# Block products for q and k of seven heads, spilled to DRAM, with the attention moved behind them

## The chip, the core and the metric

The kernel runs on one core of a Trainium2 chip. The metric is the device time of one execution in microseconds. Of the kernel before, three runs took 1871.21, 1871.85 and 1873.03 us; the median, 1871.85 us, is what changes are measured against. TensorE (PE in the profile) multiplies matrices out of SBUF into eight PSUM banks, VectorE (DVE) and ScalarE (ACT) work on tiles in SBUF and PSUM, GpSimd (POOL) does some elementwise work and issues transfers, and SyncE (SP) issues most transfers. Each engine takes its instructions in order.

## What is computed

One layer of an encoder on 512 tokens of width 2048, in float32. The part that the change concerns is the first half:

```python
h = rms_norm(x, pre_mix_g[l])
z = h @ w_in[l]                                   # 2048 x 4096: q | k | v | u, 1024 columns each
q = z[..., :ATTN_WIDTH]                           # 8 heads of 128
k = z[..., ATTN_WIDTH:2 * ATTN_WIDTH]
v = z[..., 2 * ATTN_WIDTH:3 * ATTN_WIDTH]
u = z[..., 3 * ATTN_WIDTH:]
a = chunked_attention(q, k, v, rel_bias[l])       # softmax(q k^T * scale + bias) v per head
p = multiscale_pool(u, pool_w[l], pool_scale[l])  # trailing means over 2/4/8/16, minus token, a 256 x 256 map
m = jnp.concatenate([a, p], axis=-1) @ w_o[l]
x = x + rms_norm(m, post_mix_g[l])
# then h @ w_up, a depthwise convolution, a gelu gate, @ w_down, and a second residual
```

## The kernel before

**Numbers.** Each factor of a product is split into a rounded high part and the rest (`split`, L133: the high part by ScalarE, the rest by VectorE). A product is three matmuls, high by high, high by low, low by high (`mm3`, L150). Where seven block products are used, `mm2` (L156) makes each product from a wide matmul (high of the weights by high and low of the activations, 512 columns) and a narrow one (low of the weights by high, 256 columns).

**Seven block products.** A product of two 2 x 2 block matrices needs eight block products, or seven if sums and differences of blocks are multiplied instead. The kernel before does this in the up-projection (`Factors`, `seven` and `keep`, from L1066) and in the products with w_o and w_down, but not in the projection by w_in. There the blocks are halves of the 2048 inputs, halves of the 512 tokens, and two groups of 128 output columns; the three sums of activations are made once, the sums of weights for each group of columns, by transfers that add.

**Order of the work.** TensorE's order is written out in the program; the other engines' instructions are ordered by a planner among those that are ready. `Weights` (L55) loads and splits weights in a given list, four ahead of use, into five raw tiles and eight split tiles.

1. x is loaded in 16 parts, scaled by its gain and split; q and k of head 0 are multiplied meanwhile (L335 to L349). The squares of x for the norm are summed by ScalarE and GpSimd (L365 to L373); the factor 1/rms is applied later, to the results (`R` along tokens, `rt` per token).
2. `v_group(0)` (L413): v of heads 0 to 3 as four PSUM banks of 128 tokens by 512 columns.
3. For each head h: q (`project`, L399, 48 matmuls), transposes of the softmax of an earlier head (`turn`, L462), scores of the previous head (`scores`, L437), k (48 matmuls), and values of an earlier head (`values`, L474). So between a head's scores and its transposes two projections and one head's values run. The second group of v stands at head 5.
4. Eight projections u, with the pool's running sums on VectorE (`pool_keep`, L485) and its map (`pool_mix`, L508), and the last heads' attention among them.
5. The product with w_o, the norm, then the second half of the layer.

In the softmax, VectorE adds the bias to the scores, GpSimd sets a masked corner by a memset (L450), VectorE takes the maximum, ScalarE the exponential, VectorE scales. Sums of blocks of w_o and w_down are made in DRAM by transfers spread over the stages (`sums_in_dram`, L296): plain copies on SyncE's queue, adding ones on GpSimd's queue, each waiting for the transfer that it builds on.

The rows of w_in are read where they lie: a tile for 128 columns consists of pieces of 512 bytes.

Of the kernel before, what the change touches and what calls it, by code (L numbers as in the profile page):

```python
# [54 lines left out]
class Weights:  # L55


    def __init__(self, specs, load, ahead):
        self.specs, self.load, self.ahead, self.tiles, self.used = specs, load, ahead, [], 0

    def prefetch(self, n=None):
        upto = min(len(self.specs), self.used + (self.ahead if n is None else n))
        while len(self.tiles) < upto:
            self.tiles.append(self.load(*self.specs[len(self.tiles)]))
# [11 lines left out]
def encoder_layer(ctx: ExitStack, tc: tile.TileContext, x, xT, vecs, rel, post_mix, post_ffn,  # L76
                  w_in, pool_w, w_o, w_up, w_down, out):
# [13 lines left out]
    acc = mixing.enter_context(tc.tile_pool(name="acc", bufs=1))  # L91
# [51 lines left out]
    def load_w(name, src, a, b):  # L143
        n = a * b
        raw, hi, lo = raw4(name + "r"), w4(name + "h"), w4(name + "l")
        load_w.last = nc.sync.dma_start(raw[:, :n].rearrange("p (a b) -> p a b", a=a), src).ins
# [30 lines left out]
    def new_hT(name):  # L177

        return [new_pair(f"{name}{i}", 4, S) for i in range(4)]

    def blk(hT, kb, sl=slice(None)):
        return tuple(hT[kb // 4][:, part, kb % 4, sl] for part in range(2))


# [8 lines left out]
    def g_both(gT, kb):  # L193
        v = gT[kb // 4][:, kb % 4]
        return v[:, 1:3, :].rearrange("p a b -> p (a b)"), v[:, 0:4:3, :]

# [19 lines left out]
    def halves(name, w, c0, a, b):  # L216
        n = KD // a
        return [(f"{name}_{i}", rows(w, i * a * P, c0, a, b), a, b) for i in range(n)]

    def head_cols(what, h):  # L220
        return {"q": 0, "k": ATTN, "u": 3 * ATTN}[what] + h * P

    def qk_specs(h):
        return halves(f"q{h}", w_in, head_cols("q", h), 8, P), halves(f"k{h}", w_in, head_cols("k", h), 8, P)

    def v_specs(i):
        return halves(f"v{i}", w_in, 2 * ATTN + i * 512, 2, 512)
# [26 lines left out]

    def v_and_ready_specs(g):
        specs = v_specs(g)
        for n in range(4 if g == 0 else 2):
            (cc, i), j = READY[2 * g + n // 2], n % 2
            specs.insert(3 * n + 2, (f"rw{cc}{i}_{j}", first_block(cc, i - 1, 0)[:, 2 * j:2 * j + 2, :], 2, 512))
        return specs  # L260

    def keep_ready(g, n):
        if 2 * g + n // 2 >= len(READY):
            return
        (cc, i), j = READY[2 * g + n // 2], n % 2
# [4 lines left out]
    for h in range(1, HEADS):  # L270
        q, k = qk_specs(h)
        specs += q + k
        if h == 5:
            specs += v_and_ready_specs(1)
    for g in range(4):
        for j in range(2):
            specs += halves(f"u{2 * g + j}", w_in, head_cols("u", 2 * g + j), 8, P)
        if g:
            specs += pm_spec(g - 1)
    for i in WO:  # L280
# [9 lines left out]
    weights = Weights(specs, load_w, 4)  # L290

# [34 lines left out]
    R = RR[:, 0, :]  # L326
    rt = const.tile([P, NT], F32, name="rt")
    xt = [acc8(f"xT{i}", "AABB"[i]).rearrange("p (a b) -> p a b", a=4) for i in range(4)]
    hT = new_hT("hT")
# [5 lines left out]
    for kb in range(KD):  # L335
        i, o = divmod(kb, 8)
        nc.sync.dma_start(xt[kb // 4][:, kb % 4, :], xT[kb * P:(kb + 1) * P, :])
        for what in "qk":
            if kb in chunks:
                raw, hi, lo = first[f"{what}0_{i}"]  # L340
                sl = slice(o * P, (o + chunks[kb]) * P)
                nc.sync.dma_start(raw[:, sl].rearrange("p (a b) -> p a b", b=P),
                                  rows(w_in, kb * P, head_cols(what, 0), chunks[kb], P))
                split(hi[:, sl], lo[:, sl], raw[:, sl])
        last_split = split(*blk(hT, kb), xt[kb // 4][:, kb % 4, :], col(V_PREMIX, kb))
        for what in "qk":
            _, hi, lo = first[f"{what}0_{i}"]
            sl = slice(o * P, (o + 1) * P)
            mm3(ps0[what], (hi[:, sl], lo[:, sl]), blk(hT, kb), kb == 0, kb == KD - 1)  # L349
    weights.prefetch(3)  # L350
    nc.sync.dma_start(vec[:, V_CONV:], vecs[:, V_CONV:])


# [5 lines left out]
    with tc.tile_pool(name="p1", bufs=2, reuse_waits="tile") as p1:  # L359
# [3 lines left out]
        ssum = t512("bias", bufs=1)  # L363

        with tc.issue_after(last_split):  # L365
            for kb in range(KD):
                sq = t512("tmp")
# [1120 lines left out]
```

## Time and profile before

| | |
|---|---|
| median of the runs | 1871.85 us (1871.21 to 1873.03) |
| profiled execution: time and span | 1869.37 and 1867.6 us |
| granted TensorE clock | 0.999 |
| VectorE, ScalarE, GpSimd busy | 1437.1, 1020.2, 297.8 us |
| HBM read and written | 361.44 and 96.47 MB |

The profile is one execution, taken by the hardware profiler. A page gives the busy time of each engine, the chain of work that ended last (followed back from the last instruction), and groups of instructions; other views give the timeline, the waits and tables of stretches of time. A group's row has the source line, the engine, the operation, the tile written and those read, the shape, the count, then busy time and the mean of one in ns, then the idle time before and what ended it. A timeline's row has the start and the length in us. Matmuls overlap in the pipeline, so the time of one is read from the starts of consecutive ones and not from the length in its row.

### The profile page before, as it was taken

How to read it: one execution, taken by the hardware profiler on the slowest of the kernel's cores; microseconds unless marked ns; L12 is line 12 of the kernel's file. 1: busy time of each engine (PE TensorE's matmuls, PEld its weight loads, DVE VectorE, ACT ScalarE, POOL GpSimd, SP SyncE). 2: the span in 40 equal slices, each digit the busy share in tenths (PEclk: the TensorE clock that was granted, in tenths of full speed). 3: DMA queues.
4: the chain of work that ended last, by engine and by line, in shares of the span. 5: the costliest groups of instructions: out<-in, count | busy, mean ns of one | idle time of the engine just before them, and what ended most of it. 6: DMA issues, size and time to landing. Idle time of an engine off the chain costs nothing.

```text
span 1867.6 us, 24890 instructions
## 1 busy us (share of the span) xinstructions
PE 1857.1 (99%) x9486; PEld 1590.2 (85%) x9486; DVE 1437.1 (77%) x1631; ACT 1020.2 (55%) x1287; POOL 297.8 (16%) x400
## 2 busy tenths in 40 slices
PE   9999999999999999999999999999999999999998
PEld 7888888888889888888888888888888888888886
DVE  5555445577598988888888888888887899899875
ACT  6433333346455566656666565565655665565553
POOL 4301011100000121221212212122121001111101
PEclk9999999999999999999999999999999999999999
DMA  8899599997794689898888988988889977877785
GB/s 298 248 255 233 163 253 252 246 251 255 225 306 180 184 203 206 199 205 204 201 206 194 207 208 198 208 196 207 208 174 299 352 221 174 199 206 180 173 245 143
DMA packets 181751, 409.20 MB, mean 219 GB/s; under 512 B 11456, under 2 KB 62528, under 8 KB 176320
## 3 DMA queue, kind: packets, MB, share of 16 engines
q0 software_dynamic: 52112, 156.78, 43.9%
q1 hardware_dynamic: 129520, 250.84, 40.1%
q8 instruction: 74, 1.21, 0.3%
q14 instruction: 45, 0.37, 0.1%
HBM read 361.44 MB, written 96.47 MB: 245 GB/s over the span
## 4 chain that ended last, share of the span: by engine, by line
PE 98%; DVE 1%; ACT 1%; DMA 0%; SPq 0%; issue 0%; POOL 0%; DVEq 0%; POOLq 0%; ACTq 0%
PE qa L159 16%; PE qa L165 8%; PE qg L159 8%; PE qg L165 4%; PE qd L159 4%; PE pa L153 4%; PE pa L154 4%; PE pa L151 4%; PE m L154 3%; PE m L151 3%; PE m L153 3%; PE qd L165 2%; PE pg L153 2%; PE pg L154 2%; PE pg L151 2%; PE u L151 2%
## 5 line engine op out<-in xcount | busy, mean ns | idle before, releaser
L159 PE MATMUL qa<-gT,wfh 128*128 128x512 f32 x984 | 246.4, 392 | 0.0
L135 ACT ACTIVATE wfh<-wx 128x1024 fp32r<-128x1024 f32 x164 | 173.8, 1060 | 129.0 <-PE qg L159 46.4
L136 DVE TENSOR_TENSOR wfl<-wx,wfh 128x1024 fp32r<-128x1024 f32 x164 | 200.4, 1222 | 51.7 <-ACT wfh L135 37.4
L159 PEld LDWEIGHTS qa<-gT,wfh 128*128 128x128 f32 x984 | 177.0, 189 | 31.7
L1106 POOL DMA_DIRECT2D wx<-in_w_up x122 | 104.6, 857 | 500.4 <-DVE wfl L136 464.5
L159 PE MATMUL qg<-h,wfh 128*128 128x512 f32 x656 | 162.1, 389 | 0.0
L159 PEld LDWEIGHTS qg<-h,wfh 128*128 128x128 f32 x656 | 122.9, 188 | 25.4
L136 DVE TENSOR_TENSOR bl<-b,bh 128x2048 fp32r<-128x2048 f32 x56 | 127.1, 2286 | 18.6 <-ACT bh L135 11.7
L135 ACT ACTIVATE wfh<-wy 128x1024 fp32r<-128x1024 f32 x82 | 86.9, 1060 | 93.1 <-PE qg L159 52.8
L165 PE MATMUL qa<-gT,wfl 128*128 128x256 f32 x984 | 137.7, 283 | 0.0
L135 ACT ACTIVATE bh<-b 128x2048 fp32r<-128x2048 f32 x56 | 106.1, 1913 | 57.0 <-DVE b L870 22.8
L165 PEld LDWEIGHTS qa<-gT,wfl 128*128 128x128 f32 x984 | 129.4, 191 | 3.4
L151 PE MATMUL pa<-bh,ah 128*128 128x512 f32 x320 | 124.5, 389 | 0.0
L153 PE MATMUL pa<-bl,ah 128*128 128x512 f32 x320 | 124.5, 389 | 0.0
L154 PE MATMUL pa<-bh,al 128*128 128x512 f32 x320 | 124.5, 389 | 0.0
L136 DVE TENSOR_TENSOR wfl<-wy,wfh 128x1024 fp32r<-128x1024 f32 x82 | 100.1, 1220 | 7.3 <-ACT wfh L135 3.0
L165 PEld LDWEIGHTS qg<-h,wfl 128*128 128x128 f32 x656 | 89.5, 190 | 6.4
L136 DVE TENSOR_TENSOR wfl<-wz,wfh 128x1024 fp32r<-128x1024 f32 x41 | 50.2, 1224 | 54.1 <-PE qa L159 52.8
L165 PE MATMUL qg<-h,wfl 128*128 128x256 f32 x656 | 91.5, 282 | 0.0
L159 PE MATMUL qa<-h,wfh 128*128 128x512 f32 x328 | 82.1, 392 | 0.0
L159 PE MATMUL qd<-gT,wfh 128*128 128x512 f32 x328 | 81.0, 389 | 0.0
L938 POOL DMA_DIRECT2D sum<-part x30 | 36.2, 1207 | 261.7 <-DVE part L924 190.1
(543 smaller groups left out, 4549.9 us busy)
## 6 DMA issues: line engine op xcount, KB each, us to landing
wx<-in_w_up POOLq DMA_DIRECT2D x122, 512.0 KB, 6.1
b<-in_w_down SPq DMA_DIRECT2D x32, 1024.0 KB, 7.0
wx<-in_w_up SPq DMA_DIRECT2D x43, 512.0 KB, 5.4
wz<-in_w_up SPq DMA_DIRECT2D x41, 512.0 KB, 5.7
wy<-in_w_up SPq DMA_DIRECT2D x41, 512.0 KB, 4.6
wy<-in_w_up POOLq DMA_DIRECT2D x41, 512.0 KB, 6.6
sum<-part POOLq DMA_DIRECT2D x38, 512.0 KB, 7.7
wt<-in_w_o POOLq DMA_DIRECT2D x16, 1024.0 KB, 12.8
```

Source lines behind the costliest of these rows:

```text
L135: rounded = nc.scalar.activation(hi, src, AF.Copy)
L136: rest = nc.vector.tensor_sub(lo, src, f32(hi))
L151: nc.tensor.matmul(ps, l[0], r[0], start=first, stop=False, skip_group_check=onto)
L153: nc.tensor.matmul(low, l[0], r[1], start=False, stop=False, skip_group_check=onto)
L154: nc.tensor.matmul(ps, l[1], r[0], start=False, stop=last, skip_group_check=onto)
L159: nc.tensor.matmul(ps, w[0][:, kb], pairs[kb][0], start=fresh and not kb, stop=last, skip_group_check=not fresh)
L165: nc.tensor.matmul(ps[:, sl], w[1][:, kb], pair[:, sl], start=False, stop=last, skip_group_check=not fresh)
L938: nc.gpsimd.dma_start(dest, v, accum_op=ALU.add)
L1106: nc.gpsimd.dma_start(self.raw[k, what], self.block(k, m, kh), accum_op=ALU.add)
```

## The change

- q and k of heads 1 to 7 are made by seven block products for each head; the two groups of 128 columns are q and k of the head. The activations' sums are made from x while the first group of v is multiplied. The weights' sums are made by VectorE.
- The results of a head (before the factor 1/rms) are written to DRAM (`zqk`), with k negated as the block scheme gives it; the factor is applied when they are read back, by GpSimd (`load_head`). The results of v are written and read back in the same way (`vd`), and so are the pool's results of the first three groups (`pooled`).
- All attention runs after the last block product: three heads within the second group of v, five within the projections u. The pool's running sums move from VectorE to GpSimd, and several tiles of this stage get one buffer and not two.
- The second and fourth quarter of the activations (the later half of the tokens, first half of the inputs) are overwritten by a difference during the block products and restored from x afterwards.
- w_in comes as packed blocks, so that a row of a tile lies as 4 KB in one piece.

The diff, cut; a line that is only "..." marks what is left out:

```diff
     def v_and_ready_specs(g):
...
+    READY_AT = {0: (7,), 1: (3, 4, 5, 6, 7)}
...
+    z0 = raw4("z0").rearrange("p (a b) -> p a b", a=2)
+    nc.scalar.activation(z0[:, 0], ps0["q"], AF.Copy)
+    nc.vector.tensor_scalar_mul(z0[:, 1], ps0["k"], -1.0)
+    nc.gpsimd.dma_start(zqk[0], z0)
...
+    def v_spill(i, ps):
+        for p in range(2):
+            v = raw4(f"vs{p}").rearrange("p (a b) -> p a b", a=2)
+            for t in range(2):
+                nc.scalar.activation(v[:, t], ps[2 * p + t], AF.Copy)
+            nc.gpsimd.dma_start(vd[i][:, 2 * p:2 * p + 2, :], v)
+
+    def scaled(q):
+        for kb in range(4 * q, 4 * q + 4):
...
+                    nc.scalar.activation(sq, v, AF.Square)
+                    nc.gpsimd.tensor_add(ssum, sq, ssum)
+                nc.scalar.activation(v, v, AF.Copy, scale=col(V_PREMIX, kb))
+            yield
...
+    def x_sums():
+        for i in range(2):
+            yield from scaled(2 + i)
+            yield from scaled(i)
...
+            nc.vector.tensor_sub(a22, a22, a21)
+            keep(5, a22)
+            nc.vector.tensor_sub(a21, a11, a21)
+            differences.append(a21)
+            nc.vector.scalar_tensor_tensor(a11, a22, -1.0, a11, op0=ALU.mult, op1=ALU.subtract)
+            keep(6, a11)
+            nc.vector.scalar_tensor_tensor(a12, a11, -1.0, a12, op0=ALU.mult, op1=ALU.subtract)
+            keep(3, a12)
...
+    class Pairs:
...
+        def make(self, k, i):
...
+            split(hi, lo, {3: y, 7: y, 2: z}.get(i, x))
+            if i == 1:
+                nc.vector.tensor_add(x, x, w)
+            elif i == 5:
+                nc.vector.tensor_add(x, x, y)
+            elif i == 6:
+                nc.vector.tensor_add(x, x, z)
+            elif i == 3:
+                nc.vector.tensor_add(y, y, w)
...
+    def qk_product(k, i):
+        w = pairs.get()
+        if i in FIRST:
+            qk_banks[k, BANK[i]] = bank(f"q{BANK[i]}_{k}")
+        mm2(qk_banks[k, BANK[i]], w, [factor_of(ms, i, kb) for kb in range(8)], i in FIRST, i in TURNED)
...
+        elif i == 4:
...
+            nc.vector.tensor_add(z[:, 0, :T], one[:, 0, 0], one[:, 0, 1])
+            nc.vector.tensor_add(z[:, 1].rearrange("p (a b) -> p a b", a=2), m[:, :, 0], m[:, :, 1])
+            nc.scalar.activation(z[:, 0, T:], a[:, T:], AF.Copy)
+            nc.vector.tensor_add(z[:, 0, T:], a[:, :T], z[:, 0, T:])
+            nc.gpsimd.dma_start(zqk[k + 1], z)
...
+    for k, i in [at for at in pairs.order if at[0] is not None]:
+        if k == pairs.n - 1 and i in (7, 4):
...
+            next(steps)
+        qk_product(k, i)
+        qk_keep(k, i)
...
+        if (k, i) == (pairs.n - 1, 7):
+            restore()
+        if i in (3, 7, 4) and (k, i) != (0, 3):
+            more_sums(1)
...
+        def load_head(h):
+            state["bias", h] = t512("bias", bufs=1)
+            nc.sync.dma_start(state["bias", h], rel[h])
+            v = p1.tile([P, 2, S], F32, tag="zq", bufs=1, name="zq")
+            nc.sync.dma_start(v, zqk[h])
+            nc.gpsimd.tensor_mul(v, v, RR)
+            pair = [p1.tile([P, 2, S], F32R, tag="qk" + p, bufs=1, name="qk" + p) for p in "hl"]
+            split(*pair, v)
+            state["qk", h] = [tuple(p[:, n, :] for p in pair) for n in range(2)]
...
                 nxt = p1.tile([P, WIDE], F32, tag="us", bufs=2, name="us")[:, :PAD + S]
-                nc.vector.tensor_add(nxt[:, step:], cur[:, step:], cur[:, :PAD + S - step])
+                nc.gpsimd.tensor_add(nxt[:, step:], cur[:, step:], cur[:, :PAD + S - step])
...
+        load_head(0)
+        v_load(0)
+        for h in range(3):
+            run(3 if not h else 1)
+            scores(h)
+            more_sums(1)
+            run(1)
+            if h:
+                values(h - 1)
+            more_sums(1)
+            run(2)
+            turn(h)
+        run(1)
+        v_spill(1, psv)
...
+        for j in range(8):
+            ps = project(f"u{j}", mid(2 if j == 0 else j + 1) if j not in (1, 7) else None)
+            if 1 <= j <= 5:
+                turn(j + 2)
+                if j < 5:
+                    scores(j + 3)
+            if j in (2, 4, 6):
+                pool_mix(j // 2 - 1, spill_mix)
+            if j < 7:
+                pool_keep(j // 2, j % 2, ps)
+                more_sums(2 if j == 6 else 1)
...
+    qk_blocks = w_in[0][:, :2 * ATTN].reshape(2, 8, P, 2, HEADS, P).transpose(4, 3, 0, 2, 1, 5)
```

`run(n)` advances the second v by n steps of 12 matmuls; two of its 16 steps run before the last two block products. `mid(h)` is called in the middle of a projection u and issues the values of head h (and, once, the scores of head 3).

More of the change, by code (lines that the diff above doesn't have):

```diff
@@ new lines, in encoder_layer @@
+    pairs = Pairs()
+    psv = [bank(f"v0_{t}") for t in range(NT)]
+    sums_of_x = x_sums()
+    for n, _ in enumerate(v_steps(0, psv)):
+        for _ in range(2):
+            next(sums_of_x, None)
+        if n == 9:
+            for i, v in enumerate(differences):
+                split(*(hT[i][:, :, at, :] for at in AT[1]), v)
+            early_x.close()
+            p0 = mixing_w.enter_context(tc.tile_pool(name="p0", bufs=1, reuse_waits="tile"))
+    weights.limit = len(specs)
+    psr = bank("R")
@@ L389, in encoder_layer @@
         state = {}
-        def keep(what, h, ps):
-            f = t512("tmp")
-            nc.vector.tensor_mul(f, ps, R)
-            hi, lo = t512(what + "h", F32R), t512(what + "l", F32R)
-            split(hi, lo, f)
-            state[what, h] = hi, lo
         def project(name, between=None):
```

347 lines of the change are left out of this document (213 added, 134 removed).

## The prediction

> **What bounds the kernel now.** I read the page's busy times first, then the chain that ended last, then what TensorE waited for.
>
> ```profile
> span 1867.6 us, 24890 instructions
> PE 1857.1 (99%) x9486; PEld 1590.2 (85%) x9486; DVE 1437.1 (77%) x1631; ACT 1020.2 (55%) x1287; POOL 297.8 (16%) x400
> PE 98%; DVE 1%; ACT 1%; DMA 0%; SPq 0%; issue 0%; POOL 0%; DVEq 0%; POOLq 0%; ACTq 0%
> PE q L151 <- ACT q_0h L135: 0.3, 1, 0.3
> PE q L153 <- DVE hT L139: 0.3, 1, 0.3
> ```
>
> TensorE is busy for 99% of the span, the chain is 98% TensorE, and apart from the first instruction its named waits are two of 0.3 us at the start. So time is saved only by giving TensorE fewer columns, and lost only by a new wait of TensorE. Next I look at what one head costs on TensorE now, from the timeline, and at what seven block products cost where the kernel already uses them (its up-projection), from the chain and from a table of stretches.
>
> ```profile
> 108.74 1.09 PE pt L468 x10
> 111.61 0.39 PE L151 MATMUL k<-hT,k_0h 128*128 128x512 f32 x1
> ...
> 122.51 0.39 PE L151 MATMUL a<-pth,vh 128*128 128x512 f32 x1
> ...
> 135.51 1.09 PE pt L468 x10
> ```
>
> The 48 matmuls of k take 122.51 - 111.61 = 10.90 us, 0.227 us each; q is the same work, so q and k of a head take 21.80 us. The transposes `pt` come once a head, 135.51 - 108.74 = 26.77 us apart, so one head's attention takes 26.77 - 21.80 = 4.97 us of TensorE: 1.09 the transposes, and the scores and the values, which have equal columns, 1.94 each.
>
> ```profile
> 667.44 1.91 PE qa L165 x16
> ...
> 1388.78 1.91 PE qa L165 x16
> ```
> ```profile
> core 0: us, PE busy (x) PEld busy (x) DVE busy (x) ACT busy (x) POOL busy (x), PEclk, DMA share, GB/s
> 667.40:1388.80 721.40, 721.40 (x4147) 637.13 (x4146) 600.74 (x706) 440.30 (x537) 156.06 (x186) 1.00 0.89 203
> ```
>
> In the up-projection a block of the same size as q and k of a head takes seven products of 8 wide and 8 narrow matmuls, 112 in all. The 721.4 us hold 4147 / 112 = 37 blocks, 19.50 us each, with TensorE busy throughout at clock 1.00, VectorE busy 83% and ScalarE 61%.
>
> **The change, part by part.** *The products.* Heads 1 to 7 fall from 21.80 to 19.50 us: 7 x 2.30 = 16.1 us off TensorE. Head 0, v, the pool projections u and every matmul of the attention stay, as many and as wide, so this is the whole gain. Beyond it, 4 KB rows can win at most the two waits of 0.3 us at the start, because no other wait of TensorE is a transfer; I take 0, bounds 0 and -0.6.
>
> *The sums before the products.* While v of the first four heads runs, ScalarE now squares and scales x, and splits the sums as well as the weights.
>
> ```profile
> 22.40:72.70 50.30, 50.30 (x225) 41.65 (x224) 19.87 (x17) 24.63 (x33) 29.45 (x23) 1.00 0.80 262
> L368 ACT ACTIVATE tmp<-xT 128x512 f32<-128x512 f32 x16 | 9.8, 628 | 8.3 <-POOL bias L372 8.1
> L135 ACT ACTIVATE wfh<-wx 128x1024 fp32r<-128x1024 f32 x164 | 173.8, 1060 | 129.0 <-PE qg L159 46.4
> L136 DVE TENSOR_TENSOR wfl<-wx,wfh 128x1024 fp32r<-128x1024 f32 x164 | 200.4, 1222 | 51.7 <-ACT wfh L135 37.4
> ```
>
> From the last split of x to the end of v are 50.3 us. ScalarE's list: 32 instructions of 0.63 (16 squares, 16 scalings) = 20.2; 9 weight splits, 6 splits of sums, 2 of differences and 4 of the first factors, 21 x 1.06 = 22.3; together 42.5 us, 84%. VectorE: 21 splits x 1.22 and 8 sums, costed like a split, 35.4 us. Both fit; lower bound 0. The upper: the third and fourth pieces of x must be finished before the z weights land in their place. If that is 3 us late, the second product waits 3 us. I take 0, since both engines keep over 7 us free.
>
> *The stage of the products.* Per head VectorE makes 7 splits and 4 sums of 1024 (11 x 1.22 = 13.4) and, after the products, the adds whose prices stand in these rows.
>
> ```profile
> L1182 DVE TENSOR_TENSOR z<-zm 128x512 f32<-128x512 f32 x41 | 28.3, 691 | 1.4
> L1184 DVE TENSOR_TENSOR z<-qa,z 128x256 f32<-128x256 f32 x41 | 17.1, 417 | 0.3 <-ACT z L1183 0.3
> ```
>
> That is 4 x 0.69 + 2 x 0.42 = 3.6, in all 17.0 of 19.5 us, 87%. The up-projection ran without a TensorE wait at 83%, and there the weight sums were made by transfers, here by VectorE, which shortens their chain. Cost 0. If VectorE's cover went, a head would take VectorE's time and not 19.5.
>
> *The move of the attention.* All eight heads now run in what is left of the second v (14 of its 16 steps of 12 matmuls, 14 x 2.73 = 38.2 us), the eight u (8 x 10.90) and three pool mixes (3 x 2.73): with 8 x 4.97 that is 173.4 us on TensorE. What a head's transposes wait for is its softmax, and its cover shrinks. Today two projections and one head's values, some 23.7 us, lie between a head's scores and its transposes. After the change three v steps do for head 0 (8.2 us), three steps and one head's values for heads 1 and 2 (10.1), and one u and values for heads 4 to 7 (12.8); head 3 has half a u more. I measure the softmax from the last scores matmul to the last scaling.
>
> ```profile
> 111.37 0.40 PE L154 MATMUL s<-kh,ql 128*128 128x512 f32 x1
> 138.15 0.40 PE L154 MATMUL s<-kh,ql 128*128 128x512 f32 x1
> ```
> ```profile
> 120.37 0.48 DVE L457 TENSOR_SCALAR s<-s,rs 128x512 f32<-128x512 f32 x1
> 148.21 0.49 DVE L457 TENSOR_SCALAR s<-s,rs 128x512 f32<-128x512 f32 x1
> ```
> ```profile
> 140.80 1.24 POOL L303 DMA_DIRECT2D wt<-in_w_o  x1 [25.04 <-DMA wt<-in_w_o]
> 141.54 0.92 POOL L450 MEMSET s<- 64x64 f32 x4
> ```
>
> With the next matmul issued 0.23 us later, head 1 needs 120.85 - 111.60 = 9.2 us and head 2 148.70 - 138.38 = 10.3: there GpSimd's mask memsets stood behind a DRAM sum that was waiting for a transfer. So head 0 is late by 9.2 - 8.2 = 1.0 us, and heads 1 and 2, by the dearer chain, by 0.2 each. Heads 3 to 7 have 2.5 us or more in hand: 0. Behind a waiting transpose stand the v or u matmuls and thus everything else of TensorE.
>
> GpSimd's load grows: each head's q and k times 1/rms (128x1024, reading SBUF), and the running sums of the pools.
>
> ```profile
> L372 POOL TENSOR_TENSOR bias<-tmp,bias 128x512 f32<-128x512 f32 x14 | 23.8, 1700 | 3.3 <-ACT tmp L368 2.6
> L493 DVE TENSOR_TENSOR us<-u 128x527 f32<-128x527 f32 x8 | 5.7, 707 | 0.4
> ```
>
> The multiplication isn't in the trace; twice the row gives 3.4 us. The pool sums go from 0.71 on VectorE to some 1.75 on GpSimd, 16 of them within the stage. One memset caught behind one multiplication makes the dearer chain 13.7 us: upper bounds 5.5 us for head 0, 3.6 each for heads 1 and 2, 0.9 each for 4 to 7. I stay with the measured chains.
>
> *Spills and their return.* A head's result goes out and comes back; only head 0's return is near its use.
>
> ```profile
> sum<-part POOLq DMA_DIRECT2D x38, 512.0 KB, 7.7
> bias<-in_rel SPq DMA_DIRECT2D x8, 256.0 KB, 5.8
> ```
>
> Head 0 was written long before. Its load needs room that the sums of x give up after the last 6-product, some 11 us before the last product ends, and scores(0) stands 8.2 us behind that end. Load (the slower row, 7.7), multiplication 3.4 and split 2.3 make 13.4 of 19.2 us: 0. If the load had to wait for the last head's spill (adds of z 1.5, spill 7.7, then 13.4), scores(0) would be 22.6 - 8.2 = 14.4 us late; that is the upper bound. The spills, the packed loads and the reload of half of x add transfers to queues that TensorE does not wait for today.
>
> *The sum.* 1869.37 (the profiled run, 1.8 above its span) - 16.1 + 1.0 + 0.4 = 1854.7. The median of the runs, 1871.85, lies 2.5 above that run: **1857.2 us**.
>
> [...] Some of this slows where GpSimd and VectorE overlap, and the trace shows it:
>
> ```profile
> L372 POOL TENSOR_TENSOR bias<-tmp,bias x14: 1288/1598/2244, 25.7 to 53.0; 128x512 f32<-128x512 f32 x14
> 33.44 1.49 DVE L136 TENSOR_TENSOR v_2l<-v_2r,v_2h 128x1024 fp32r<-128x1024 f32 x1 [2.79 <-ACT v_2h L135]
> 53.20 2.18 DVE L136 TENSOR_TENSOR rw_0l<-rw_0r,rw_0h 128x1024 fp32r<-128x1024 f32 x1 [2.79 <-ACT rw_0h L135]
> ```
>
> The same GpSimd add takes 1.29 to 2.24 us, and a split beside it up to 2.18 where 1.22 is usual. [...]
>
> **The rivals.** *One, VectorE becomes the bound in the attention stage.*
>
> ```profile
> L452 DVE TENSOR_REDUCE nm<-s 128x1 f32<-128x128 f32 (+3 forms) x32 | 15.0, 470 | 5.0 <-POOL s L450 5.0
> L136 DVE TENSOR_TENSOR ptl<-pt,pth 128x512 fp32r<-128x512 f32 (+3 forms) x32 | 14.2, 483 | 0.1
> L448 DVE SCALAR_TENSOR_TENSOR s<-s,bias 128x128 f32<-128x128 f32 (+3 forms) x32 | 14.0, 480 | 0.0
> L457 DVE TENSOR_SCALAR s<-s,rs 128x128 f32<-128x128 f32 (+3 forms) x32 | 12.2, 382 | 0.3
> ```
>
> These four groups are 55.4 us for eight heads; eight splits of q and k 9.8, 29 weight splits 35.4, and some 27 for pools, v and x (an estimate from the same prices by size): about 128 of 173.4 us. GpSimd's reads are 8 x 3.4 + 16 x 1.75 = 55 us. If every one stopped VectorE, VectorE would need 183 us, 10 more than TensorE: 1871.85 - 16.1 = 1855.8 is the time without a wait, so 1855.8 + 10 = 1866, and up to 1870 with late softmaxes. For it: the 2.18. Against: the 17 VectorE instructions of the stretch from 22.4 to 72.7 us, in which those adds ran, took 19.87 us, 1.17 each, no more than a split alone.
>
> *Two, head 0's return is late* by the bound above: 1855.8 + 14.4 = 1870.2, or about 1864 for half of it. For it speaks that space is tight and loads share one queue; against, the 5.8 us in hand.
>
> *Three, slower: the softmax is held up by GpSimd at every head.* Its four memsets are short but in order with multiplications, pool sums and DRAM sums. With three of them behind 1.75 us each the chain is 9.2 + 5.3 = 14.5 us, and TensorE waits 6.3 + 4.4 + 4.4 + 4 x 1.7 = 21.9 us: 1855.8 + 21.9 = 1877.7. It decides against the change from a chain of some 13.5 us. For it: head 2's four memsets in a row. Against: one such case cost 1.1 us, not 5.3.
>
> *Four, the seven products bring nothing*, because VectorE's 17.0 us a head stretch to 21.8: 1872. Against it speaks the up-projection's stretch.
>
> **How the numbers follow.** The forecast's case (waits of 0 to 6 us in all, 1854 to 1862) gets 0.56, rivals one and two 0.12 each, three 0.14, four 0.06. About 0.2% (3.7 us) is what a measurement of this kernel can tell from no change. Faster (below 1868.1) are the forecast, rival two and 0.07 of rival one, together 0.75; the rest of one and all of four are the same, 0.11; slower 0.14. The range starts at 1854.2 (no wait, the start's 0.6 us gained, 1 us of scatter) and ends at 1870.5, which leaves out rival three, rival four and the worst of the others.
>
> **What would show it.** Right: per head 112 matmuls in 19.5 us without gaps in the stage of the products; VectorE there near 87%; TensorE's waits of about 1 us before head 0's transposes and almost none later; a GpSimd multiplication of about 3.4 us. Wrong: product periods over 20 us, waits of the scores for the split of q and k (rival two), waits of the transposes at most heads with memsets behind GpSimd work (three), splits of 2 us and more all through the u stage (one). More than 6 us of such waits refutes the sum.

## The result, and the profile after

The changed kernel takes 1963.69 us (median of four runs, 1958.3 to 1965.19) against 1871.72 us (four runs beside them): 1.0485 times the time before, with a 95% interval of 1.0464 to 1.0506. The forecast was 1857.2 us, faster. The first view is the page of the changed kernel: busy times, TensorE's busy tenths and its granted clock in 40 slices of 49 us, and the chain.

```profile
span 1960.8 us, 25466 instructions
PE 1865.3 (95%) x9598; PEld 1598.1 (81%) x9598; DVE 1530.2 (78%) x1704; ACT 1083.5 (55%) x1376; POOL 357.0 (18%) x446
PE   9977947979999999999999999999999999999998
...
PEclk9988968989999999999999999999999999999999
...
PE 79%; DMA 7%; DVE 6%; issue 3%; ACT 2%; POOL 2%; SPq 0%; DVEq 0%; POOLq 0%; ACTq 0%
```

TensorE now stands still for 1960.8 - 1865.3 = 95.5 us, where it was 10.5. Nearly all of it lies in the slices 3 to 11, the stage that the change rewrote, and there the granted clock falls as well, to the digit 6 in the sixth slice. The chain, which was 98% TensorE, holds 7% of transfers and 6% of VectorE. The stretches of the rewritten stage show where (the columns after the range: length, busy us of each engine with its instructions, granted clock, share of the DMA engines, GB/s):

```profile
80.00:240.00 160.00, 136.44 (x748) 117.86 (x747) 108.58 (x116) 67.03 (x82) 18.38 (x19) 0.94 0.89 248
240.00:290.00 50.00, 21.08 (x93) 17.52 (x92) 19.90 (x34) 14.69 (x25) 7.99 (x41) 0.71 0.85 263
290.00:400.00 110.00, 98.66 (x468) 83.38 (x468) 73.10 (x137) 49.76 (x95) 33.39 (x45) 0.93 0.78 241
400.00:440.00 40.00, 29.54 (x149) 25.53 (x148) 23.55 (x47) 14.66 (x31) 13.52 (x22) 0.87 0.88 226
440.00:550.00 110.00, 103.07 (x447) 83.91 (x446) 72.50 (x92) 56.16 (x75) 23.94 (x34) 0.97 0.73 220
550.00:1940.00 1390.00, 1387.27 (x7300) 1196.38 (x7299) 1159.84 (x1195) 818.92 (x971) 227.81 (x260) 1.00 0.83 211
```

So 23.6 us are lost in the block products (80 to 240), 28.9 where the attention begins, 28.7 in the rest of the attention and at w_o, and 2.7 behind. What TensorE waited for (total, times, longest):

```profile
PE s L156 <- ACT qkh L138: 28.2, 1, 28.2
PE pt L688 <- DVE s L677: 20.1, 4, 10.5
PE qg L170 <- DVE wfl L139: 8.9, 1, 8.9
PE qa L170 <- DVE wfl L139: 8.8, 1, 8.8
```

**The sum that closes.** TensorE's full-clock work fell by 7 x (21.80 - 19.57) = 15.6 us (the 19.57 is measured further down). At full clock it would be busy for 1857.1 - 15.6 = 1841.5 us; it was busy for 1865.3. The other 23.8 are what is left over; they are put down to the lowered clock, 0.71 to 0.97 in the stretches above up to 550 us. Together -15.6 + 85.0 more idle + 23.8 = +93.2 us, which is the difference of the spans, 1960.8 - 1867.6.

**First place: z, between two heads.** This is the timeline of the changed kernel between heads 1 and 2 of the products (start, length, engine, line, operation, output from inputs, in brackets the idle time ahead and what ended it).

```profile
107.21 0.42 DVE L566 TENSOR_TENSOR z<-qa,z 128x256 f32<-128x256 f32 x1
...
113.31 1.24 POOL L309 DMA_DIRECT2D wt<-in_w_o  x1 [13.38 <-DMA wt<-in_w_o]
114.05 1.07 POOL L567 DMA_DIRECT2D zqk<-z  x1
...
127.11 0.43 DVE L563 TENSOR_TENSOR z<-za 128x256 f32<-128x256 f32 x1 [18.35 <-DMA zqk<-z]
...
130.04 1.06 ACT L138 ACTIVATE wfh<-wx 128x1024 fp32r<-128x1024 f32 x1 [11.47 <-DVE wx L466]
```
```profile
DVE z L563 <- DMA zqk<-z: 59.8, 6, 18.4
```

The head's last add into z (L566) is done at 107.6. Its spill is the next thing for GpSimd, but GpSimd stands in an adding transfer of the w_o sums that waits 13.38 us for a copy, so the spill is issued at 114.05. The first add of the next head into z (L563) needs only `za`, which exists early, so the planner put it behind L566 with a single split between. But z has one buffer: VectorE stops at L563 until the spill has landed, 18.35 us, and with it all splits and sums of weights behind it (ScalarE's next split waits 11.47 us for such a sum). Then TensorE has no factors. Six waits of this kind take 59.8 us.

**Second place: the beginning of the attention.**

```profile
268.82 1.06 ACT L138 ACTIVATE v_0h<-v_0r 128x1024 fp32r<-128x1024 f32 x1 [18.09 <-DMA rw01h<-rw_1h]
...
272.14 0.38 SPq L150 DMA_DIRECT2D rw_1r<-in_w_down  x1
...
273.11 0.78 SPq L637 DMA_DIRECT2D zq<-zqk  x1
...
281.07 2.33 POOL L638 TENSOR_TENSOR zq<-zq,RR 128x1024 f32<-128x1024 f32 x1 [6.01 <-DMA zq<-zqk]
...
283.44 1.06 ACT L138 ACTIVATE qkh<-zq 128x1024 fp32r<-128x1024 f32 x1 [7.83 <-POOL zq L638]
```

ScalarE wants to split a weight of v and waits 18.09 us for a split tile that a factor of w_down ("ready" factor, `rw`) holds until its spill to DRAM has landed. Five halves of such factors now stand one behind another in the second half of v. SyncE takes loads in order, so head 0's reload (`zq`, 273.11) stands behind raw loads (272.14, the issue before it at 257.92) whose tiles the stalled engines hold. It lands 8 us later, GpSimd multiplies, ScalarE splits, and the scores start after a stop of 28.2 us.

**Third place: the pool's results.**

```profile
413.60 0.69 ACT L738 ACTIVATE mx<-pm,vec 128x512 f32<-128x512 f32 x1 [10.28 <-DMA pooled<-mx]
...
414.84 3.26 DVE L139 TENSOR_TENSOR pm1l<-pm1r,pm1h 128x512 fp32r<-128x512 f32 x1 [10.10 <-ACT pm1h L138]
415.18 2.36 POOL L638 TENSOR_TENSOR zq<-zq,RR 128x1024 f32<-128x1024 f32 x1
...
418.21 0.49 DVE L677 TENSOR_SCALAR s<-s,rs 128x512 f32<-128x512 f32 x1
...
418.75 1.75 PE L688 MATMUL pt<-ident,s 128*128 128x128 f32 x7 [10.46 <-DVE s L677]
```

ScalarE waits 10.28 us for the one tile `mx`, whose last content is still on its way to DRAM. A head's last exponential stands behind it, and its transposes start 10.46 us late. Not all of that stop is the landing: VectorE's split of the pool's weights (`pm1l`) takes 3.26 us beside GpSimd's multiplication, where a split of this shape takes 0.68 at 402.69 us, and the scaling ahead of the transposes stands behind it. That is about 2.6 us, an estimate from these two rows.

The three have one form: a tile with few buffers is written to DRAM, an engine that works in order must write that tile again, and everything behind that instruction waits for the landing.

### The profile page after: what moved, and what is told of

Read it like the earlier page. It is cut to its first block, busy times and chain, and to the rows that moved or that the text cites. A ratio compares the mean times of both kernels' runs of the same rounds, so it can differ in the third digit from the quotient of the medians.

```text
span 1960.8 us, 25466 instructions
## 1 busy us (share of the span) xinstructions
PE 1865.3 (95%) x9598; PEld 1598.1 (81%) x9598; DVE 1530.2 (78%) x1704; ACT 1083.5 (55%) x1376; POOL 357.0 (18%) x446
## 4 chain that ended last, share of the span: by engine, by line
PE 79%; DMA 7%; DVE 6%; issue 3%; ACT 2%; POOL 2%; SPq 0%; DVEq 0%; POOLq 0%; ACTq 0%
PE qa L164 15%; PE qa L170 8%; PE qg L164 8%; PE qg L170 4%; PE qd L164 4%; PE pa L156 4%; PE pa L159 4%; PE pa L158 4%; PE m L158 2%; PE m L159 2%; PE m L156 2%; PE qd L170 2%; DMA zqk<-z 2%; PE pg L156 2%; PE pg L159 2%
## 5 line engine op out<-in xcount | busy, mean ns | idle before, releaser
L138 ACT ACTIVATE wfh<-wx 128x1024 fp32r<-128x1024 f32 x192 | 203.5, 1060 | 163.1 <-PE qg L164 52.1
L164 PE MATMUL qa<-gT,wfh 128*128 128x512 f32 x1152 | 290.3, 394 | 0.0
L139 DVE TENSOR_TENSOR wfl<-wx,wfh 128x1024 fp32r<-128x1024 f32 x192 | 234.5, 1221 | 51.0 <-ACT wfh L138 36.7
L164 PEld LDWEIGHTS qa<-gT,wfh 128*128 128x128 f32 x1152 | 208.7, 190 | 37.5
L170 PE MATMUL qa<-gT,wfl 128*128 128x256 f32 x1152 | 163.1, 285 | 9.8 <-DVE wfl L139 8.8
L170 PEld LDWEIGHTS qa<-gT,wfl 128*128 128x128 f32 x1152 | 153.0, 193 | 14.5 <-issue 9.0
L138 ACT ACTIVATE wfh<-wy 128x1024 fp32r<-128x1024 f32 x96 | 101.8, 1061 | 110.5 <-PE qg L164 59.8
L139 DVE TENSOR_TENSOR wfl<-wy,wfh 128x1024 fp32r<-128x1024 f32 x96 | 117.1, 1219 | 7.6 <-ACT wfh L138 3.2
L164 PE MATMUL qd<-gT,wfh 128*128 128x512 f32 x384 | 95.0, 389 | 1.6 <-ACT wfh L138 1.6
L164 PEld LDWEIGHTS qd<-gT,wfh 128*128 128x128 f32 x384 | 72.0, 188 | 16.8 <-ACT wfh L138 1.8
## 6 DMA issues: line engine op xcount, KB each, us to landing
wt<-in_w_o POOLq DMA_DIRECT2D x16, 1024.0 KB, 13.5
```

Source lines behind the costliest of these rows:

```text
L138: rounded = nc.scalar.activation(hi, src, AF.Copy)
L139: rest = nc.vector.tensor_sub(lo, src, f32(hi))
L164: nc.tensor.matmul(ps, w[0][:, kb], pairs[kb][0], start=fresh and not kb, stop=last, skip_group_check=not fresh)
L170: nc.tensor.matmul(ps[:, sl], w[1][:, kb], pair[:, sl], start=False, stop=last, skip_group_check=not fresh)
```

## The experiments

The theory: these waits for landings are the loss, and landings are long because 1 MB transfers (the sums of blocks of w_o and w_down in DRAM) fill the DMA engines and GpSimd's queue. Its rivals: VectorE's load, the packed rows, the block products themselves, or the sums in DRAM alone.

**The queue of the spills.** In the first kernel SyncE issues the spill of z, in the second all spills.

```diff
-            nc.gpsimd.dma_start(zqk[k + 1], z)
+            nc.sync.dma_start(zqk[k + 1], z)
```

> Only the spill of a head's z is issued by SyncE, not by GpSimd. Theory Q (spills stand in GpSimd's queue behind the adding DRAM sums, and VectorE waits in order for the single z buffer): the waits of VectorE for the spill (59.8 us in six waits) fall below 15 us, the heads in the stage of the products come every 19.5 to 20.5 us, and the time falls by 30 to 45 us, to 1918 to 1935 us. Rival V (VectorE's own list of 17.0 us a head is too long once it waits for ScalarE and transfers): the heads stay near their present mean of some 25 us and the time changes by less than 5 us. Rival T (transfers as a whole are saturated, whatever the queue): the spill lands as late from SyncE, and the time falls by at most 10 us.

> All spills (z of all heads, v, the ready factors rw, the pool's results) are issued by SyncE; GpSimd issues only the adding DRAM sums. Theory Q: the wait of 28 us before head 0's scores and the wait of 10.5 us behind the pool's results go too; 1858 to 1885 us. Rival V: above 1940. Rival T: 1920 to 1955, with spills that land in 10 us and more.

The first took 1949.5 us, ratio 1.0419 (1.0389 to 1.045), the second 1928.4, ratio 1.0307 (1.0277 to 1.0336). Both miss the ranges of theory Q; the first gained somewhat more than rival T allowed, the second lies in T's range. VectorE's waits for z fell from 59.8 to 43.3 and 43.7 us, no further: the issue is prompt now, but in the second kernel the landing itself took between 4.0 and 20.4 us. GpSimd's queue was about a quarter of these waits.

**The sums of w_o out of the way.** In one kernel the sums are issued only behind the products, up to four at a place; in another they are left out and plain blocks of w_o are read in their place, so its result is another one. The same omission is made in the kernel before.

```diff
-        if i in (3, 7, 4) and (k, i) != (0, 3):
-            more_sums(1)
...
-                more_sums(2 if j == 6 else 1)
+                more_sums(4 if j == 6 else 4)
```
```diff
-                    step(wo_sum[i][cc][:, sl, :], source[:, sl, :])
```

> Spills stay on GpSimd's queue; the DRAM sums of w_o that were issued between the block products are issued behind them instead, up to four at a place, in the attention stage. Theory Q: the stage of the products runs at 19.5 to 20.5 us a head and the spill of z lands in 4 to 6 us; what the crowded sums cost in the attention stage is open (the whole may be 1900 to 1980). Rival V: the heads stay at some 25 us. Rival T: the stage of the products gets faster too, since its traffic falls, but the spills land late again wherever the sums now are.

> The changed kernel without the DRAM sums of w_o: the transfers that make them are left out, and the products with w_o read plain blocks of w_o in their place (so four of the seven w_o factors are other numbers). Theory S (the 1 MB sums keep the transfer engines full, spills and loads land in 8 to 20 us, and engines that wait for them in order stop TensorE): every wait of the first 500 us shrinks to a few us, 1856 to 1870 us. Rival V (VectorE's load) or rival O (the order of the attention, whose softmax has too little cover): over 1900 us, with the waits of the transposes as they are.

> Control: the same omission in the kernel before. Theory S: there no engine waits in order for a spill, so the sums cost TensorE nothing: 1869 to 1873 us.

The same 140 us in three kernels, in this order: before, changed, changed without these sums.

```profile
80.00:220.00 140.00, 140.00 (x667) 117.94 (x666) 76.32 (x145) 51.12 (x95) 14.91 (x32) 1.00 0.87 232
```
```profile
80.00:220.00 140.00, 119.48 (x659) 103.67 (x658) 92.06 (x98) 59.99 (x73) 16.55 (x17) 0.93 0.94 263
```
```profile
80.00:220.00 140.00, 140.00 (x795) 122.50 (x795) 116.45 (x131) 74.20 (x94) 4.80 (x9) 1.00 0.41 142
```

Without the sums the products run without a gap, 795 matmuls where 659 ran, and VectorE is 83% busy. So neither its load nor the products are at fault. With the sums only moved behind the products, nothing left out, TensorE is busy for the whole of this stretch too (797 matmuls). The median landing of z's spill, in the list of DMA issues of the changed kernel and of the one without sums (KB, us to landing):

```profile
zqk<-z POOLq DMA_DIRECT2D x8, 512.0 KB, 10.4
```
```profile
zqk<-z POOLq DMA_DIRECT2D x8, 512.0 KB, 4.8
```

VectorE still waits for each landing there, 19.8 us in six, but 4.4 at most, and the four factors made ahead hide that. The median landing is this short only where no sums of w_o run among the products (DMA share 0.41 in both kernels): 3.9 us with the sums moved, 4.8 without them. With the sums running (share 0.94) the 10.4 us are over twice as long.

The kernel without sums took 1909.64 us, ratio 1.0204 (1.0174 to 1.0233). That is far above theory S (1856 to 1870) and in the range of its rivals, although rival V is refuted by the stretch above: two fifths of the loss stay, most of it in the beginning of the attention (16.0 us) and at the transposes (15.9). Before, leaving them out changes nothing: 1872.38 us in one run against 1870.91. There the same transfers land as slowly (a median of 12.8 us for an adding one, 13.5 after), but nothing waits for one behind which TensorE's work stands. The kernel with the sums moved is the worst, 1986.51 us in one run and just above the range expected: the transfers then fall on the attention (DMA share 1.02 from 300 to 500 us), where transposes wait 60.8 us:

```profile
PE pt L686 <- DVE s L675: 60.8, 12, 33.7
```

**The packed rows alone**, put into the kernel before.

```diff
-        return halves(f"v{i}", w_in, 2 * ATTN + i * 512, 2, 512)
+        return [(f"v{i}_{c}", w_v[i, c], 2, 512) for c in range(8)]
```

> The kernel before with one part of the change alone: w_in in packed blocks, rows of 4 KB. The prediction says 0 to -0.6 us: 1871 to 1873 us, with a lower share of the transfer engines between 100 and 400 us. If row size bore on the path, the time would change by over 3 us.

1870.89 us against 1871.64, ratio 0.9996 (0.9985 to 1.0007): no effect.

**Another tile, or another order, for z.** In one kernel z comes out of the ring of raw weight tiles. In the other z keeps its one buffer, and only the order is changed: the next head's first add into z stands behind that head's add for product 7.

```diff
-            z = p0.tile([P, 2, S], F32, tag="z", bufs=1, name="z")
+            z = raw4("z").rearrange("p (a b) -> p a b", a=2)
```
```diff
+            qk_keep.seven = nc.vector.tensor_add(v, qk_z.pop((k, "5")), v).ins
...
-            nc.vector.tensor_add(z[:, 0, :T], one[:, 0, 0], one[:, 0, 1])
+            with tc.issue_after(qk_keep.seven):
+                nc.vector.tensor_add(z[:, 0, :T], one[:, 0, 0], one[:, 0, 1])
```

> The changed kernel with z in the ring of five raw tiles, so that the next head's z needs not wait for the spill. Theory S with its wait at the single z: VectorE's waits for the spill (59.8 us) fall below 10 us and the stage of the products takes 19.5 to 21 us a head; the waits behind it stay; 1915 to 1935 us. If the loads of the weights are late by themselves under the sums, the heads stay above 22 us and the time above 1940 us.

> One edge of order alone: VectorE's first add into z is put behind this head's add for product 7, where the planner had put it directly behind the last add of the head before. Same buffers, same queue, same traffic. Theory S with the place of the add as what turns a late landing into a stop of VectorE: the waits for the spill fall from 59.8 to below 10 us, heads of 19.5 to 21 us, 1915 to 1935 us. If the queue or the traffic alone did it, the waits move and the time changes by less than 10 us.

The ring helped little: 1949.1 us in one run, and VectorE still waits 46.2 us in four, presumably since the ring's slots are held by landings and loads as well. The products are no faster for it (617 matmuls in the 140 us, where the changed kernel has 659); the gain lies at head 0, whose named wait is 5.1 us and not 28.2. The one edge of order gave 1930.78 us, ratio 1.0317 (1.0284 to 1.0349), 33 us less than the changed kernel with the same instructions and bytes. The same 140 us, and VectorE's waits for the spill:

```profile
80.00:220.00 140.00, 135.65 (x762) 117.50 (x761) 109.03 (x118) 67.69 (x86) 18.05 (x19) 0.99 0.99 286
```
```profile
DVE z L564 <- DMA zqk<-z: 31.2, 4, 8.1
```

TensorE is busy for 135.65 us, although the spills' median landing is no better (13.4 us): the landings didn't get shorter, but less stands behind them. The time is in the theory's range, the waits are not: they fell to 31.2 us, not below 10, and the factors made ahead cover most of what is left.

**The beginning of the attention.** From here each kernel contains the later add. One has a single ready factor in place of three; the next has the sums of w_o left out besides.

```diff
-    READY = (0, 1), (1, 1), (0, 2)
+    READY = ((0, 1),)
...
-    READY_AT = {0: (7,), 1: (3, 4, 5, 6, 7)}
+    READY_AT = {0: (7,), 1: (7,)}
```

> The kernel with the later add (1930.8 us), with one w_down factor made ready in DRAM in place of three: one ready load in the second half of v in place of five, so ten spills fewer and five raw loads fewer stand ahead of head 0's reload. Theory (the split tiles that the ready factors' spills hold stop ScalarE, VectorE and SyncE's loads, head 0's reload among them): the wait ahead of head 0's scores falls from 24.4 us to below 8, and the time to 1905 to 1915 us, less what the two factors cost later in the w_down stage. Rival (the reload is late because the sums in DRAM fill the DMA engines): that wait stays above 18 us and the time at 1925 to 1935 us.

> The same with the sums of w_o in DRAM left out (plain blocks of w_o are read in their place; the sums for w_down remain). Theory (waits for landings, in engines that take their work in order): head 0's wait below 6 us, the stage of the products at 19.5 us a head, the waits of the transposes still 10 to 16 us for the single mx tile and the late softmaxes; 1880 to 1892 us. Rival (something else than landings costs the rest): the time stays within 10 us of the 1909.6 us of the kernel without w_o sums.

With fewer ready factors it is 1916.81 us, ratio 1.0235 (1.0218 to 1.0252): 14 less, and head 0's wait falls from 24.4 to 17.4 us, neither below 8 as the theory had it nor above 18 as the rival had it. The timeline of this kernel shows what took over:

```profile
237.10 0.58 POOL L568 DMA_DIRECT2D zqk<-z  x1 [7.37 <-DVE tmp L617]
...
247.58 0.40 POOL L609 MEMSET recip<- 128x16 f32 x4 [9.89 <-DMA zqk<-z]
...
248.71 2.73 POOL L639 TENSOR_TENSOR zq<-zq,RR 128x1024 f32<-128x1024 f32 x1
...
252.58 0.58 PE L156 MATMUL s<-qkh 128*128 128x256 f32 x1 [17.38 <-ACT qkh L138]
```

GpSimd must first set `recip`, which lies in the memory of the products' closed tiles, and that memory is held by the last head's z until its spill has landed. Head 0's multiplication stands behind it. With the sums left out too it is 1899.85 us (1.0139 to 1.0171), 8 above the range expected and within the rival's: the wait for `mx`, 9.9 us ahead of the transposes, and 8.8 us at head 0 were still there.

**Other queues for the reload and for `mx`**, and then all moves together (later add, all spills by SyncE, one ready factor, reload by ScalarE).

```diff
-            nc.sync.dma_start(v, zqk[h])
+            nc.scalar.dma_start(v, zqk[h])
...
-            nc.gpsimd.dma_start(pooled[:, kb - HEADS, :], v)
+            nc.sync.dma_start(pooled[:, kb - HEADS, :], v)
```

> The kernel with the later add (1930.8 us), with the reloads of q and k issued by ScalarE and the spills of mx by SyncE; nothing else moved. Theory (head 0's reload is late because it stands on SyncE's queue behind raw loads that wait for tiles; exp waits for mx because its spill stands on GpSimd's queue): the wait ahead of head 0's scores falls by the reload's share of it, from 24.4 to 12 to 18 us, the ready factors' part remaining; the transposes' waits fall from 18.4 to below 10 us; 1908 to 1920 us. Rival (both are late by the transfers' own times, whatever queue issues them): no wait changes by more than 4 us, 1926 to 1936 us.

> All moves together: the later add, every spill on SyncE, one ready factor, the reloads of q and k issued by ScalarE. Theory: each takes a wait of its own away; the stage of the products near 19.5 us a head, head 0's wait below 6 us, transposes below 12 us in all; 1885 to 1900 us. Rival (the waits replace one another, as every landing takes 8 to 20 us while the sums run): 1910 us and more, TensorE's idle time over 50 us in all.

The queues alone gave 1922.2 us, 9 less but not the 11 to 23 expected: head 0 still waits 19.6 us, and a new wait of 11.9 appears at the transposes, where VectorE stands 10.3 us at the split of a ready factor, released by nothing that the profile names. All moves together gave 1894.59 us, ratio 1.0123 (1.0108 to 1.0138), inside the theory's range; head 0 still waits 11.5 us, where below 6 was expected, the transposes 3.1 in all.

**Head 0 early, then `mx` by ScalarE.** Head 0's q and k go into a raw tile before the second half of v begins; the next kernel also has ScalarE issue the spills of `mx`, and makes its ready half five steps earlier.

```diff
+        if (k, i) == (pairs.n - 1, 3):
+            zq0 = raw4("zq0").rearrange("p (a b) -> p a b", a=2)
+            nc.scalar.dma_start(zq0, zqk[0])
+            nc.gpsimd.tensor_mul(zq0, zq0, RR)
```
```diff
-    READY_AT = {0: (7,), 1: (7,)}
+    READY_AT = {0: (7,), 1: (2,)}
...
-            nc.sync.dma_start(pooled[:, kb - HEADS, :], v)
+            nc.scalar.dma_start(pooled[:, kb - HEADS, :], v)
```

> All moves (1894.6 us) and one more: head 0's q and k are reloaded into a tile of the raw weights' ring and multiplied by R already at the last head's product 3, two products before the second half of v. Theory (the rest of head 0's wait, 11.5 us, is its reload behind other work, and TensorE's clock falls only because it stands still): the wait falls below 5 us, the granted clock between 230 and 260 us rises from 0.67 to 0.85 and more, and the time to 1878 to 1886 us. Rival (head 0's split waits for the memory of the products' closed pool, held by head 7's spill until it has landed): the wait stays above 8 us and the time within 5 us of 1894.6.

> The same with the second ready half made at the second half of v's third product in place of its eighth, and the spills of mx issued by ScalarE. Theory (the single mx tile is late because its spill stands behind loads in SyncE's queue): TensorE's waits between 400 and 440 us fall from 7.4 to below 3 us, 3 to 8 us off the time of the kernel with head 0 early. Rival (the spill's landing itself takes 6 to 10 us while the first sums run): these waits stay above 6 us, no more than 2 us either way.

The first is a miss in an instructive form: 1895.61 us, no gain. The wait for `qkh` is gone and the granted clock from 230 to 260 us rose from 0.67 to 0.85, both as the theory had it, but 3.8 us at the next scores, 3.2 at `qkl`, 4.0 more at the transposes and 1.6 more at w_o have come. The second took 1883.8 us, ratio 1.0064 (1.0048 to 1.0081): TensorE's idle time from 400 to 440 us fell from 7.5 to 3.3. The 11.8 us gained are more than the 3 to 8 expected, and more than these 4.2 us of waits explain. What each of its two edits gave wasn't tried apart.

**What is left.** The last kernel with the sums of w_o left out, and with four of their steps moved away from the beginning of the attention.

```diff
-        if i in (3, 7, 4) and (k, i) != (0, 3):
+        if i in (3, 7, 4) and (k, i) != (0, 3) and k < pairs.n - 1:
...
-                more_sums(2 if j == 6 else 1)
+                more_sums(2 if j in (0, 1, 2, 3, 6) else 1)
```

> The last kernel (1883.8 us) with the sums of w_o in DRAM left out (plain blocks of w_o are read in their place). Its TensorE is idle for 30.3 us and busy for 1851.1, against 1841.0 (1857.1 of before less 16.1) at full clock. Theory (what is left are landings of 8 to 12 us under the sums, and the clock that falls behind each stop): the waits between 226 and 260 us go, the granted clock there rises above 0.9, and the time falls to 1866 to 1874 us, 14 to 28 above the 1855.8 of the forecast's sum without waits less what the first sums still cost. Rival (something that is no landing costs the rest): 1880 us and more.

> The last kernel (1883.8 us) with four steps of the sums moved from the end of the products and head 0 into the projections of u, nothing left out. Theory: the bias that head 0's softmax waits for (issued at 226.2 us, 12 us to landing) and the last spill land sooner, the waits between 226 and 260 us (7.8 us with the slow clock behind them 5.1 more) fall by half; the moved sums fall into a stretch whose engines are full already (share 1.0 to 1.1 from 340 to 400 us) and give back a part: 1876 to 1884 us. Rival (the sums only wait in another place): 1884 to 1895 us, with new waits of the transposes behind 300 us.

Without the sums: 1877.51 us, ratio 1.0034 (1.0024 to 1.0044), 3.5 above the theory's range and below the rival's. With some moved: 1884.38, no change; the waits from 230 to 260 us fell from 7.8 to 2.2, and 2.9 appeared from 340 to 380 us, where the engines' share is 1.08. The heads' starts in the kernel without sums give the period of the products:

```profile
92.70 1.98 PE L164 MATMUL qd<-gT,wfh 128*128 128x512 f32 x8
...
190.53 1.98 PE L164 MATMUL qd<-gT,wfh 128*128 128x512 f32 x8
```
```profile
PE m L158 <- DVE wo_0l L139: 3.5, 1, 3.5
PE pt L695 <- DVE s L684: 2.4, 2, 1.4
PE s L158 <- DVE qkl L139: 1.6, 1, 1.6
PE s L156 <- ACT qkh L138: 1.5, 1, 1.5
PE pd L158 <- DVE bl L139: 1.5, 1, 1.5
```

Five heads in 97.83 us are 19.57 each. The largest waits that remain are single ones of 1.0 to 3.5 us: at w_o, two at head 0's scores, two ahead of its transposes, and `pd`, the first down-projection, a wait that the kernels with a single ready factor share.

The sum closes here too. TensorE is idle for 1875.7 - 1852.1 = 23.6 us, 13.1 more than before, and busy for 10.6 us more than the 1841.5: -15.6 + 13.1 + 10.6 = +8.1 us, the difference of the spans. Most of it is no longer in the rewritten stage: the up-projection starts 2.9 us later than in the kernel before (first `up` at 566.56 against 563.66 us), but the product with w_down takes 5.0 us longer (from the first `pa` to the first `yl` 385.81 us against 380.80). That stage took 380.8 to 384.7 us in the kernels with three ready factors and 384.2 to 385.8 with one; why it varies wasn't tried. No version of the changed kernel beat the kernel before.

## Why the prediction was wrong

- **The step that failed** is the one on spills and their return, priced at 0: "The spills, the packed loads and the reload of half of x add transfers to queues that TensorE does not wait for today." That TensorE doesn't wait for these queues today says nothing of a tile that is spilled. The new spills, and old ones moved next to new work, created the waits themselves: VectorE at z (59.8 us), ScalarE at a split tile (18.1) and at `mx` (10.3). Most of the 85.0 us by which TensorE stands idle longer lie behind these. The one edge of order ahead of the add into z is worth 33 us by itself.
- "Only head 0's return is near its use" looked at the reading side. The writing side was near: between z's last add and the next write into it VectorE has one split, 1.22 us. Even for head 0 the bound of 14.4 us was passed (28.2). The bound let the load wait for the last head's spill alone, at 7.7 us, a row from another stage. Here the two spills of a ready factor took 15.4 and 12.6 us to land, the first issued behind an adding transfer that had waited 15.46 us, and the load stood in SyncE's queue behind a raw load that they held up. The prediction had a row of just such a queue (GpSimd's adding transfer, 25.04 us of waiting) and charged it to memsets alone.
- "If VectorE's cover went, a head would take VectorE's time and not 19.5" was the right kind of warning with the wrong cause. VectorE's load was not the trouble (83% without the sums against the 87% forecast); it stood still.
- **The clock was not in the sum**: 23.8 us of the loss are not idle time but put down to matmuls at a lowered clock behind such stops (0.71 from 240 to 290 us).
- **Right**: the products' size (19.57 against 19.50 us a head), no effect of the packed rows, and a softmax chain a little over its cover (in the kernel with all moves and no sums the transposes wait 2.4 us, all of it at head 0, against 1.4 forecast). The sums of x cost the second product 1.6 us, within the bound of 3.
- **The rivals**: the second, head 0's return late, named one of the places at half its price (14.4 against 28.2). The first, GpSimd stopping VectorE, shows in single instructions: the split of 3.26 us above, and scalings of 2.40 and 2.64 us at 343 and 386 us beside multiplications of 2.40 us each, where 0.49 is usual. That every read of GpSimd stops VectorE for its whole length, as the rival's 183 us suppose, was the author's assumption; no run shows it. But VectorE did not become the bound: with all moves and no sums TensorE is busy for the whole of 300 to 400 us, VectorE for 67.9. The third, GpSimd's memsets, held VectorE for 4.3 us in four waits of the changed kernel; no run shows a stop of TensorE that comes from it. With all moves and no sums the named waits of the attention are 5.5 us in all. The fourth, products that bring nothing, is refuted by the 19.57 us a head.
- **Still open**: how the 11.8 us between the kernel with head 0 early and the next one divide between the ready half and `mx`, where the 5.0 us in the product with w_down come from, and what the attention would take if z, `mx` and the split tiles had another buffer each, which wasn't tried.

## What to carry to other kernels

For every tile that is written to DRAM and has one buffer, write down who writes it next, how soon, and what stands behind that instruction on its engine; the landing, at its slowest in that stage, is then a latency on that engine (here up to 18.35 us on VectorE at z). Before adding a spill to a queue, look at what the queue's other transfers wait for: here 1 MB sums that cost nothing before took the median landing of one spill from 4.8 to 10.4 us. Where there is no other buffer, moving the overwriting instruction back behind work that is due earlier adds no instruction and no byte; it gained 33 us here, about as much as moving all spills to another queue (35).

## What the runs showed of the hardware

A stop of TensorE can cost more than its length; here one of 3.65 us cost 1.7 us more. From the timeline of the kernel with head 0 early and `mx` by ScalarE:

```profile
226.17 0.28 PE L156 MATMUL s<-qkh 128*128 128x256 f32 x1
230.10 0.39 PE L158 MATMUL s<-qkl,qkh 128*128 128x256 f32 x1 [3.65 <-DVE qkl L139]
...
231.92 0.63 PE L159 MATMUL s<-qkh,qkl 128*128 128x512 f32 x1
232.34 0.63 PE L156 MATMUL v<-v_6h,gT 128*128 128x512 f32 x1
232.77 0.63 PE L158 MATMUL v<-v_6l,gT 128*128 128x512 f32 x1
...
235.42 0.39 PE L159 MATMUL v<-v_6h,gT 128*128 128x512 f32 x1
```

Behind a stop of 3.65 us the matmuls first run at full speed for 1.5 us (those of 256 columns start 0.12 us apart); then, from 231.6 to 235.2 us, those of 512 columns start 0.43 us apart instead of 0.23, and then 0.23 us apart again: 1.7 us lost on top of the stop. The slow stretch is 3.6 us long, the matmuls in it are 1.9 times as far apart, and the granted clock from 230 to 260 us is 0.77.

GpSimd's multiplication of 128x1024 took 2.33 us in the second place above and up to 3.37 elsewhere in the changed kernel (at 328.77 us), where the forecast had estimated 3.4.
